# FFN in passes of three and six blocks, with gate and up of the six as seven half-size products of float16 pairs

## The chip, the cores and the metric

One core of one Trainium2 chip runs the whole program. The metric is device time in microseconds (us) of one launch; beside it a profile of one execution gives the span from the first to the last instruction and every instruction in it. The engines are TensorE (PE: matmuls, PEld: its weight loads), VectorE (DVE), ScalarE (ACT), GpSimd (POOL) and SyncE (SP, which here mostly issues DMAs).

## The reference

One step of a hybrid backbone: a layer with an attention head group and an mLSTM head group side by side, one output projection, then a SwiGLU FFN. There are 1152 tokens: 128 of context and 1024 latent. They make nine blocks of 128 rows; D_MODEL is 1024 and D_FF is 2816.

```python
def swiglu(h, w_gu, w_down):
    g, u = jnp.split(h @ w_gu, 2, axis=-1)
    return (jax.nn.silu(g) * u) @ w_down

# trunk_layer, cut
mix = jnp.concatenate([attn_o, hm], axis=-1) @ w_out
x = x + g1 * mix
h2 = rmsnorm(x, norm2_w) * (1 + sc2) + sh2
x = x + g2 * swiglu(h2, w_gu, w_down)
# and at the end
y = rmsnorm(x, final_norm_w)
```

Attention has 8 query heads of 64 and 2 key heads; a latent token reads 1152 keys, a context token 128. The inputs and outputs are float32.

## The kernel before

**Precision.** A float32 product is made of three matmuls on pairs: an operand is split into a high part and a low part, and high x high, high x low and low x high are added in PSUM. In the FFN and the output projection both parts are float32r; in the input projections they are float16.

**Tiling.** The nine blocks go through the FFN in three passes ("chunks" c = 0, 1, 2) of CB = 3 blocks, 384 tokens (CT). D_FF is cut into 22 slices f of 128. For a slice, `gate_up` loads two pieces of weights of 128x1024 (`load_piece`: DMA into `raw`, ACT casts the high part `whi` at L163, DVE subtracts for the low part `wlo` at L141), and for each runs 8 x 3 matmuls with 384 columns (L1436 to L1438). ACT (tanh) and DVE (L1455, L1456) form silu(g) * u, which is split into `hl`. `down` follows each group of slices (GROUPS): for each half n of the 1024 outputs, weight pieces of two slices each and three matmuls of 512 columns a slice and block (L1192 to L1194); the result goes through `add_gated` (two DVE operations of 512, L1181 and L1182) onto the rows `x1`. So every FFN weight is loaded and split three times, once a pass.

**Beside the passes.** Attention of chunk c + 1 runs woven into the pass of chunk c. A head is six score matmuls S (L1112) into one PSUM buffer of three banks, a maximum on DVE (L1114), an exponent on ACT (L1115), a float16 high part on ACT (L1118) and low part on DVE (L1119), two DMA transposes on SP's queue, and, for two heads at a time, value matmuls (L1136, L1137). `attn_out` applies the attention half of the output projection (8 pieces of `w_out` in two passes, 4 each; 72 matmuls), and `norm2` normalises, transposes and splits the next chunk's features during the last `down` of a pass. Before the first pass `prefill` does the mLSTM half of the output projection for all nine blocks, with part of chunk 1's attention woven in. The last group's `down_last` normalises each block as soon as it is complete and stores it.

**What sets the order.** Each engine executes its own instructions in the order of the program; that order is fixed before by a scheduler that takes the written order as priorities, `hot(n)` raising some, and readiness by a timeline. `weave(main, side, n_main, n_side)` draws n_side steps of a side generator evenly over n_main units of the main one. Buffers rotate by tag: `raw` has two, the split pieces five pairs (tags wl, ipair1, ipair0, iraw0, wq), PSUM four banks for general use (`bank`), one for values and three for S.

Of the kernel before, what the change touches and what calls it, by code (L numbers as in the profile page):

```python
# [19 lines left out]
P = 128  # L20
# [17 lines left out]
LAST = [(0, 5), (5, 5), (10, 4), (14, 4), (18, 4)]  # L38
PAIRS = [(0, 1), (2, 3), (4,), (5, 6), (7, 8)]
NG = 4  # L40
# [6 lines left out]
def hybrid_step(ctx: ExitStack, tc: tile.TileContext, I: dict, O: dict):  # L47
# [98 lines left out]
    def load_piece(srcs, shape, raw=None, own=None):  # L146
# [7 lines left out]
        raw = wp.tile([P, 1024], F32, name=nm("raw"), tag="iraw1", bufs=2) if raw is None else raw  # L154
        if not own:
            loaded["n"] = (loaded["n"] + 1) % 5
            tag = ("wl", "ipair1", "ipair0", "iraw0", "wq")[loaded["n"]]
            at = homes.get(tag, wp)
            own = [at.tile([P, 1024], F32R, name=nm(t), tag=tag, bufs=2) for t in ("whi", "wlo")]
# [4 lines left out]
        sub(lo[:, :n], raw[:, :n], hi[:, :n].bitcast(F32), "dve")  # L164
        return view(hi), view(lo)
# [253 lines left out]
    hp = ctx.enter_context(tc.tile_pool(name="hpk", bufs=1, side="right", reuse_waits="tile"))  # L419
# [644 lines left out]
    ap = ctx.enter_context(tc.tile_pool(name="ap", bufs=1, side="right", reuse_waits="tile"))  # L1064
    ap2 = ctx.enter_context(tc.tile_pool(name="ap2", bufs=1, side="right", reuse_waits="tile"))
    psum["S"] = ctx.enter_context(tc.tile_pool(name="pS", bufs=1, space=PSUM, reuse_waits="tile"))
    es_d = ExitStack()
    for name, bufs in (("mm", 3), ("wi", 2)):
        psum[name] = (ctx if name == "mm" else es_d).enter_context(tc.tile_pool(name="p" + name, bufs=bufs, space=PSUM, reuse_waits="tile"))
# [84 lines left out]
    def a_tiles():  # L1154
        return (hp.tile([P, KD, CT], F32R, name=nm("aTh"), tag="b2"),
                hp.tile([P, KD, CT], F32R, name=nm("aTl"), tag="b3"))

    def new_x1(c):
        x1 = (hp if c == 1 else rowp).tile([P, CB, D], F32, name=nm("x1"), tag="b5" if c == 1 else "b4")
        for i in range(CB):  # L1160
            if c == 2:
                dma(x1[:, i, :], x1_d[i])
        return [x1[:, i, :] for i in range(CB)]
# [11 lines left out]
    def t2():  # L1175
        return ft.tile([P, 512], F32, name=nm("t2"), tag="t2", bufs=3)
# [31 lines left out]
    def out_gates():  # L1208
        gs = []
        for n in range(2):  # L1210
            gl = xg.tile([P, 512], F32, name=nm("gl"), tag=("gl", "gx")[n], bufs=1)
            dma(gl, g_d[0, 1:2, n * 512 : (n + 1) * 512].to_broadcast([P, 512]))
            gs.append(gl)
# [161 lines left out]
    def attn_out(a, oT, gs):  # L1375

        ws = [out_pieces(0, n) for n in range(2)]
        x1 = a["x1"]
# [307 lines left out]
```

## Time and profile before

| what | value |
|---|---|
| median of 3 runs | 1529.32 us (1527.43 to 1531.47) |
| span of the profiled execution | 1523.0 us |
| PE busy, share of the span | 1466.2 us, 96% |
| DVE busy | 1017.2 us, 67% |
| ACT busy | 771.3 us, 51% |
| POOL busy | 268.0 us, 18% |
| granted TensorE clock, mean | 0.994 |

The profiled execution is known by its span; a time of its own besides is not listed, and the runs' median lies 6.3 us above the span. Busy times are sums over an engine's instructions; a matmul's busy time overlaps that of the next, so that the step between starts, not the busy time, tells its pace. In the slices of the page each digit is the busy share of a fortieth of the span in tenths. A row of the groups gives the line, engine, operation, tiles, shapes and count, then busy time, mean ns of one, and the idle time before with what ended it. A row of windows gives the window, its length, then each engine's busy time (and count), the granted clock, the DMA engines' share and GB/s; with one line chosen, only that line's busy time stands there.

### The profile page before, as it was taken

The page shows a single profiled execution, that of the slowest core. Times are in us where ns is not written, and L with a number is a line of the kernel's source. Part 1 is how long each engine was busy: PE and PEld are TensorE (multiplying, and loading weights), DVE is VectorE, ACT ScalarE, POOL GpSimd, SP SyncE. Part 2 cuts the span into 40 slices and gives each one's busy share as a digit, 9 for nine tenths or more (in the row PEclk, how much of TensorE's full clock was granted, in tenths as well). Part 3 has the DMA queues.
Part 4 walks back from the last instruction along what each step waited for, and adds up shares of the span by engine and source line. Part 5 has one row for each costly group of instructions (what it writes and reads, how often), then busy time and mean ns, then how long its engine had stood idle before and what let it go on. Part 6 is the DMA issues. An engine that isn't in the chain of part 4 may idle for free.

```text
span 1523.0 us, 23411 instructions
## 1 busy us (share of the span) xinstructions
PE 1466.2 (96%) x8539; PEld 1239.4 (81%) x8539; DVE 1017.2 (67%) x2021; ACT 771.3 (51%) x1433; POOL 268.0 (18%) x354
## 2 busy tenths in 40 slices
PE   6889999999998899999999999999999999999997
PEld 3635667677776789989998999989998989999996
DVE  4979555838567966877647487787866585554554
ACT  4855576847654644646433344656553443323333
POOL 0122422333344531000010100100010101101110
PEclk9999999999999999999999999999999999999998
DMA  9575223523465676878635366986864455543541
GB/s 368 162 224 189 73 70 42 123 55 78 104 187 189 149 195 176 197 168 192 166 113 164 125 206 192 198 183 143 193 145 140 137 153 172 153 141 123 152 144 56
DMA packets 386665, 233.77 MB, mean 153 GB/s; under 512 B 169142, under 2 KB 345478, under 8 KB 386550
## 3 DMA queue, kind: packets, MB, share of 16 engines
q1 hardware_dynamic: 384414, 228.62, 55.3%
q10 hardware_dynamic: 2008, 3.26, 1.0%
q8 instruction: 67, 1.10, 0.3%
q14 instruction: 48, 0.39, 0.1%
q0 software_dynamic: 128, 0.39, 0.1%
HBM read 182.21 MB, written 11.69 MB: 127 GB/s over the span
## 4 chain that ended last, share of the span: by engine, by line
PE 59%; DVE 2%; DMA 1%; ACT 0%; issue 0%; SPq 0%; DVEq 0%
PE mm L1438 11%; PE mm L1437 11%; PE mm L1436 11%; PE mm L1192 5%; PE mm L1193 5%; PE mm L1194 5%; PE S L1112 3%; PE po L1137 1%; PE po L1136 1%; DMA plT<-pl 1%; PE mm L1224 1%; PE mm L1220 1%; PE mm L1222 1%; DVE t L1181 0%; DVE x L1182 0%; PE mm L120 0%
## 5 line engine op out<-in xcount | busy, mean ns | idle before, releaser
L163 ACT CAST whi<-raw 128x1024 fp32r<-128x1024 f32 x214 | 219.1, 1025 | 365.7 <-PE mm L1437 129.8
L141 DVE TENSOR_TENSOR wlo<-raw,whi 128x1024 fp32r<-128x1024 f32 x214 | 257.7, 1204 | 176.0 <-ACT whi L163 173.0
L1437 PE MATMUL mm<-aTl,whi 128*128 128x384 f32 x1056 | 354.4, 336 | 0.0
L1438 PE MATMUL mm<-aTh,wlo 128*128 128x384 f32 x1056 | 354.2, 336 | 0.0
L1436 PE MATMUL mm<-aTh,whi 128*128 128x384 f32 x1056 | 353.2, 335 | 0.0
L141 POOL TENSOR_TENSOR hl<-tn,hl 128x384 fp32r<-128x384 f32 x66 | 83.5, 1267 | 848.6 <-ACT hl L1459 792.4
L1436 PEld LDWEIGHTS mm<-aTh,whi 128*128 128x128 f32 x1056 | 198.3, 188 | 0.7
L1437 PEld LDWEIGHTS mm<-aTl,whi 128*128 128x128 f32 x1056 | 198.3, 188 | 0.6
L1438 PEld LDWEIGHTS mm<-aTh,wlo 128*128 128x128 f32 x1056 | 198.3, 188 | 0.4 <-issue 0.4
L1192 PE MATMUL mm<-whi,hl 128*128 128x512 f32 x372 | 144.4, 392 | 1.1 <-DVE t L1181 1.1
L1193 PE MATMUL mm<-wlo,hl 128*128 128x512 f32 x372 | 145.1, 391 | 0.0
L1194 PE MATMUL mm<-whi,hl 128*128 128x512 f32 x372 | 142.7, 391 | 0.0
L1119 DVE SCALAR_TENSOR_TENSOR pl<-pr,st,ph 128x1152 f16<-128x1152 f32 (+1 forms) x72 | 98.0, 1361 | 37.1 <-ACT ph L1118 37.0
L1114 DVE TENSOR_REDUCE st<-S 128x1 f32<-128x1152 f32 (+1 forms) x72 | 88.9, 1234 | 16.8 <-PE S L1112 16.5
L1115 ACT ACTIVATE pr<-S,st 128x1152 f32<-128x1152 f32 (+1 forms) x72 | 81.3, 1129 | 35.0 <-DVE st L1114 30.8
L1118 ACT ACTIVATE ph<-pr,st 128x1152 f16<-128x1152 f32 (+1 forms) x72 | 83.8, 1164 | 26.5 <-issue 10.7
L510 PE MATMUL wi<-headw,hT 128*128 128x384 f16 x288 | 93.9, 326 | 0.2 <-ACT th L800 0.2
L511 PE MATMUL wi<-headw,hT 128*128 128x384 f16 x288 | 93.9, 326 | 0.0
L512 PE MATMUL wi<-headw,hT 128*128 128x384 f16 x288 | 93.9, 326 | 0.0
L1181 DVE TENSOR_TENSOR t<-mm,gl 128x512 f32<-128x512 f32 x102 | 69.1, 686 | 36.8 <-PE mm L1194 17.7
L1112 PE MATMUL S<-kst,qT 128*128 128x384 f32 (+1 forms) x400 | 84.5, 344 | 0.8 <-ACT pr L1115 0.8
L1192 PEld LDWEIGHTS mm<-whi,hl 128*128 128x128 f32 x372 | 69.9, 188 | 15.2 <-DVE t L1181 1.5
(401 smaller groups left out, 2588.6 us busy)
## 6 DMA issues: line engine op xcount, KB each, us to landing
raw<-in_w_gu_dram SPq DMA_DIRECT2D x132, 512.0 KB
raw<-in_w_down_dram SPq DMA_DIRECT2D x60, 512.0 KB
a<-in_w_ada_dram SPq DMA_DIRECT2D x24, 512.0 KB
gl<-g_d SPq DMA_DIRECT2D x36, 256.0 KB
iraw<-in_w_in_dram SPq DMA_DIRECT2D x32, 256.0 KB
x<-in_x_sample_dram SPq DMA_DIRECT2D x11, 512.0 KB
raw<-in_w_out_dram SPq DMA_DIRECT2D x10, 512.0 KB
aw<-in_w_ada_dram SPq DMA_DIRECT2D x8, 512.0 KB
```

The costliest lines, as they stand in the source:

```text
L141: (dve if eng == "dve" else pool).tensor_tensor(out=out, in0=full, in1=hi, op=ALU.subtract)
L163: nc.scalar.copy(hi[:, :n], raw[:, :n])
L510: mm(ps[:, :n], ah, wh[:, k % 2, c0 : c0 + n], start=(k == 0), stop=False)
L511: mm(ps[:, :n], ah, wl[:, k % 2, c0 : c0 + n], start=False, stop=False)
L1112: mm(S[:, n, 0:w], qT[:, h, :], kst[kv][:, t, c0 + n * w : c0 + (n + 1) * w], start=(t == 0), stop=(t == 1))
L1119: dve.scalar_tensor_tensor(out=plv, in0=prv, scalar=st[:, 3:4], in1=phv, op0=ALU.mult, op1=ALU.subtract)
L1192: mm(ps, ah, wh[:, k % 2, :], start=(k == 0), stop=False)
L1193: mm(ps, ah, wl[:, k % 2, :], start=False, stop=False)
L1194: mm(ps, al, wh[:, k % 2, :], start=False, stop=(k == nk - 1))
L1436: mm(ps, wh[:, k, :], th[:, k, :], start=(k == 0), stop=False)
L1437: mm(ps, wh[:, k, :], tl[:, k, :], start=False, stop=False)
L1438: mm(ps, wl[:, k, :], th[:, k, :], start=False, stop=(k == KD - 1))
```

## The change

The three passes become two: the first of three blocks as before, and one of six (chunks 1 and 2 together, `SIX` = groups of 4, 4, 4, 4, 3, 3 slices).

- **Seven products.** For a slice, gate and up weights are cut along their 1024 inputs into halves and make a 2x2 block matrix (A11 and A12 of gate, A21 and A22 of up); the features of chunk 1 (B11, B21) and chunk 2 (B12, B22) make the other. `pair6` computes the 2x2 product from seven half-size products (4 steps of 128 inputs x 3 matmuls, 384 columns) instead of eight, with sums of weights (`weights6`, on DVE) and sums of features (`features6`) formed before, and sums of results after, some of them by adding a product onto a bank that already holds one (products 4, 5, 6 onto banks a, d, c).
- **Float16 pairs.** Both operands of these products are scaled by powers of two and split into float16 parts. The features' scale comes from the modulation (`six_scales`), that of the weights from the sums of absolute values taken by ACT for every piece in the first pass (`tally`), reduced in `weight_scale` between the passes.
- **Attention of six beside the first pass.** `attention_side` runs chunk 1's rest, its `attn_out`, chunk 2's attention and its `attn_out`, woven over the first three groups (12 slices) of the first pass (NG is 3; 92 steps instead of 50). `features6` for six blocks is woven into the last two groups (10 slices).
- **Buffers.** The attention pools are closed before the six-block pass; then `Bt` holds the features, `A4` (seven tiles) the weight pairs, `raw` has four tiles and the split down pieces four pairs; all eight PSUM banks serve `bank`. `down6` and `down_last` go over six blocks; gate vectors g2 are loaded once.

```diff
-LAST = [(0, 5), (5, 5), (10, 4), (14, 4), (18, 4)]
+SIX = [(0, 4), (4, 4), (8, 4), (12, 4), (16, 3), (19, 3)]
+PRODUCTS = ((A11, B11), (S2, T2), (S1, T1), (S3, T3), (A12, B21), (S4, B22), (A22, T4))
-NG = 4
+NG = 3
...
+        if tally is not None:
+            jk = ft.tile([P, D], BF16, name=nm("jk"), tag="t2", bufs=4)
+            act(jk[:, :n], raw[:, :n], AF.Abs, accum_out=wsum[:, tally : tally + 1])
...
+    def weight_scale():
+        dve.tensor_reduce(out=six[:, 7:8], in_=wsum, axis=AX.X, op=ALU.max)
+        emit(power_scale(fp, ones, six[:, 7:8], six[:, 2:4]))
+        dve.tensor_tensor(out=six[:, 4:5], in0=six[:, 1:2], in1=six[:, 3:4], op=ALU.mult)
...
+    def features6(a, c, i, Bt, firsts):
...
+        first = firsts.pop(0)
+        T = sp.tile([P, 4, 4, P], F32, name=nm("T"), tag="S", bufs=1)
+        with hot(600):
+            dve.tensor_tensor(out=T[:, T1], in0=first[:, 0:4], in1=F[:, 0:4], op=ALU.subtract)
+            dve.tensor_tensor(out=T[:, T2], in0=F[:, 4:8], in1=T[:, T1], op=ALU.add)
+            dve.tensor_tensor(out=T[:, T3], in0=F[:, 0:4], in1=F[:, 4:8], op=ALU.subtract)
+            dve.tensor_tensor(out=T[:, T4], in0=first[:, 4:8], in1=T[:, T2], op=ALU.subtract)
...
+    def weights6(f):
...
+        S = sp.tile([P, 4, 512], F32, name=nm("S"), tag="S", bufs=1)
+        dve.tensor_tensor(out=S[:, 1], in0=u[:, 0], in1=u[:, 1], op=ALU.add)
+        dve.tensor_tensor(out=S[:, 0], in0=u[:, 0], in1=g[:, 0], op=ALU.add)
+        dve.tensor_tensor(out=S[:, 2], in0=S[:, 1], in1=g[:, 0], op=ALU.add)
+        dve.tensor_tensor(out=S[:, 3], in0=S[:, 2], in1=g[:, 1], op=ALU.add)
+        ops = {}
+        for names, v in (((A11, A12), g), ((S2, S4), S[:, 2:4]), ((S3, S1), S[:, 0:2]), ((A22,), u[:, 1:2])):
+            n = len(names)
+            t = a4p.tile([P, 2, 2, 512], F16, name=nm("A"), tag="A4", bufs=7)
+            act(t[:, 0:n, 0], v, AF.Copy, scale=six[:, 2:3])
+            dve.scalar_tensor_tensor(out=t[:, 0:n, 1], in0=v, scalar=six[:, 2:3], in1=t[:, 0:n, 0], op0=ALU.mult, op1=ALU.subtract)
...
+    def pair6(f, Bt, acts):
+        ops = weights6(f)
+        a, b, c, d = (bank()[:, 0:CT] for _ in range(4))
+        def product(n, ps, first):
+            (wh, wl), bt = ops[PRODUCTS[n][0]], Bt[:, PRODUCTS[n][1]]
+            for k in range(4):
+                mm(ps, wh[:, k], bt[:, 0, k], start=first and k == 0, stop=False, skip_group_check=True)
+                mm(ps, wh[:, k], bt[:, 1, k], start=False, stop=False, skip_group_check=True)
+                mm(ps, wl[:, k], bt[:, 0, k], start=False, stop=k == 3, skip_group_check=True)
...
+        product(0, a, True)
+        nc.scalar.copy(p1, a)
+        product(1, b, True)
+        dve.tensor_tensor(out=u2, in0=b, in1=p1, op=ALU.subtract)
+        product(2, d, True)
+        product(3, c, True)
+        dve.tensor_tensor(out=u3, in0=c, in1=u2, op=ALU.add)
+        dve.tensor_tensor(out=c22, in0=u3, in1=d, op=ALU.subtract)
+        product(4, a, False)
+        act(tn[:, 0], a, AF.Tanh, scale=six[:, 5:6])
+        product(5, d, False)
+        dve.tensor_tensor(out=gb, in0=d, in1=u2, op=ALU.subtract)
+        act(tn[:, 1], gb, AF.Tanh, scale=six[:, 5:6])
+        dve.scalar_tensor_tensor(out=tn[:, 1], in0=tn[:, 1], scalar=1.0, in1=c22, op0=ALU.add, op1=ALU.mult)
+        dve.tensor_tensor(out=tn[:, 1], in0=tn[:, 1], in1=gb, op=ALU.mult)
+        product(6, c, False)
+        dve.tensor_tensor(out=c21, in0=c, in1=u2, op=ALU.add)
+        dve.scalar_tensor_tensor(out=tn[:, 0], in0=tn[:, 0], scalar=1.0, in1=c21, op0=ALU.add, op1=ALU.mult)
+        dve.tensor_tensor(out=tn[:, 0], in0=tn[:, 0], in1=a, op=ALU.mult)
+        act(hl[:, 0], flat, AF.Copy, scale=six[:, 6:7])
+        dve.scalar_tensor_tensor(out=hl[:, 1], in0=flat, scalar=six[:, 6:7], in1=hl[:, 0].bitcast(F32), op0=ALU.mult, op1=ALU.subtract)
...
+    def down6(x1, acts, f0, nf, gs):
+        for n in range(2):
+            pieces = down_pieces6(f0, nf, n)
+            for i in range(2 * CB):
+                ps = bank()
+                down_block6(ps, pieces, acts, i)
+                add_gated(x1[i], ps, gs[n], n)
...
+    def attention_side():
+        yield from six_scales()
+        yield from att
+        yield from attn_out(nxt, oT, lambda: row_pair(g_d[0, 1]))
+        o2 = []
+        yield from attention(2, o2, set())
+        yield from attn_out(far, o2, lambda: row_pair(g_d[0, 1]))
+    main = groups(0, cur, GROUPS[:NG])
...
+    side = attention_side()
+    weave(main, side, 18 * sum(nf for _, nf in GROUPS[:NG]) - 24, 92)
+    emit(side)
+    es_att.close()
...
+    main = groups(0, cur, GROUPS[NG:])
+    weave(main, feats, 18 * sum(nf for _, nf in GROUPS[NG:]), 40)
+    emit(feats)
+    weight_scale()
...
+    for f0, nf in SIX:
+        acts = []
+        for f in range(f0, f0 + nf):
+            for _ in pair6(f, Bt, acts):
+                if f > 0:
+                    next(done6, None)
+        if (f0, nf) != SIX[-1]:
+            emit(down6(x6, acts, f0, nf, gs6))
+        else:
+            down_last(x6, acts, f0, nf, gs6)
```

280 lines of the change are left out of this document (190 added, 90 removed).

## The prediction

> **What bounds the kernel now.** I read the page's busy shares first, then its slices, then windows over the stages.
>
> ```profile
> PE 1466.2 (96%) x8539; PEld 1239.4 (81%) x8539; DVE 1017.2 (67%) x2021; ACT 771.3 (51%) x1433; POOL 268.0 (18%) x354
> ...
> PE   6889999999998899999999999999999999999997
> DVE  4979555838567966877647487787866585554554
> ```
>
> PE has work in nearly every slice; DVE is second, and uneven. Where the change lies, I cut the span at the first gate and up matmuls of each pass. Windows over the three stages, and one inside the second (PE, PEld, DVE, ACT, POOL busy, granted clock, DMA share, GB/s):
>
> ```profile
> 560.00:889.00 329.00, 328.43 (x1810) 303.78 (x1809) 220.09 (x312) 151.89 (x199) 30.31 (x24) 1.00 0.65 166
> 889.00:1235.00 346.00, 343.21 (x1915) 316.51 (x1913) 253.83 (x377) 174.33 (x234) 27.35 (x22) 1.00 0.67 168
> 1235.00:1523.00 288.00, 276.83 (x1467) 260.23 (x1467) 156.03 (x225) 99.66 (x137) 28.61 (x22) 0.99 0.45 138
> 930.00:1140.00 210.00, 207.76 (x1204) 191.95 (x1203) 162.59 (x226) 119.03 (x155) 16.52 (x13) 1.00 0.77 174
> ```
>
> One gate and up line, 352 matmuls in each pass:
>
> ```profile
> 560.00:889.00 329.00, 118.27 (x352) 1.00 0.65 166
> 889.00:1235.00 346.00, 117.63 (x352) 1.00 0.67 168
> 1235.00:1523.00 288.00, 117.30 (x352) 0.99 0.45 138
> ```
>
> The score matmuls, six a head:
>
> ```profile
> 450.00:560.00 110.00, 10.06 (x48) 1.00 0.65 178
> 560.00:889.00 329.00, 19.83 (x96) 1.00 0.65 166
> 889.00:1235.00 346.00, 29.67 (x144) 1.00 0.67 168
> ```
>
> PE idles only 963 - 948.5 = 14.5 us after 560 us, most of it in the tail. So PE bounds all three passes. At six S matmuls a head, chunk 1's attention does 8 of its 24 heads before 560 and 16 in the first pass; chunk 2's 24 lie in the second pass; the third pass is FFN alone.
>
> A busy PE row overstates a matmul, so I take the step from start to start: float32r with 384 columns (first and last of 17 rows), float16 with 384 columns (of 21), and float32r with 512 columns (of 24).
>
> ```profile
> 1339.80 0.33 PE L1437 MATMUL mm<-aTl,whi 128*128 128x384 f32 x1
> 1342.58 0.33 PE L1438 MATMUL mm<-aTh,wlo 128*128 128x384 f32 x1
> ```
> ```profile
> 324.81 0.33 PE L512 MATMUL wi<-headw,hT 128*128 128x384 f16 x1
> 328.06 0.33 PE L511 MATMUL wi<-headw,hT 128*128 128x384 f16 x1
> ```
> ```profile
> 1495.83 0.39 PE L1524 MATMUL mm<-whi,hl 128*128 128x512 f32 x1
> 1501.09 0.39 PE L1526 MATMUL mm<-whi,hl 128*128 128x512 f32 x1
> ```
>
> The steps are 2.78/16 = 173.7 ns, 3.25/20 = 162.5 ns and 5.26/23 = 229 ns. A pass is 1056 x 0.1737 + 396 x 0.229 = 183 + 91 = 274 us of PE; of it one f (a 128-wide slice of D_FF) is 12.5 us. The second pass's other 69 of 343 us are attention: 16.5 us are the 72 output projection matmuls, 2.6 us the transposes of norm2 (24 at an estimated 0.11), and 50 are 24 heads, 2.1 us each.
>
> **The change, part by part.**
>
> *Gate and up of six blocks.* Before, 2 x 1056 = 2112 matmuls at 173.7 ns, 366.9 us. After, per f seven products of 4 x 3 = 84 matmuls, 1848 in all, in float16 with the same 384 columns: 300.3 us. So -66.6 us, of which 264 fewer matmuls make 45.9 and the shorter step 20.7. The down products stay 792 matmuls.
> The step is bounded by 162.5 ns (the row of the same shape and type, with nothing between its matmuls) and by float32r's own 173.7; I take the first.
>
> *DVE beside it.* These rows give the prices.
>
> ```profile
> L141 DVE TENSOR_TENSOR wlo<-raw,whi 128x1024 fp32r<-128x1024 f32 x202 | 249.5, 1235 | 162.2 <-ACT whi L163 159.2 <-PE mm L1224 2.4
> L1119 DVE SCALAR_TENSOR_TENSOR pl<-pr,st,ph 128x1152 f16<-128x1152 f32 x64 | 94.9, 1483 | 35.1 <-ACT ph L1118 35.0
> L1114 DVE TENSOR_REDUCE st<-S 128x1 f32<-128x1152 f32 x64 | 86.6, 1353 | 13.7 <-PE S L1112 13.5
> L1181 DVE TENSOR_TENSOR t<-mm,gl 128x512 f32<-128x512 f32 x102 | 69.1, 686 | 36.8 <-PE mm L1194 17.7 <-DMA gl<-g_d 10.4 <-PE mm L1526 6.5
> L1182 DVE TENSOR_TENSOR x<-x,t 128x512 f32<-128x512 f32 x72 | 48.7, 687 | 0.7
> L1455 DVE SCALAR_TENSOR_TENSOR tn<-tn,mm 128x384 f32<-128x384 f32 x66 | 36.4, 552 | 54.2 <-PE mm L1438 54.0
> L235 DVE SCALAR_TENSOR_TENSOR ipair<-iraw,isc,ipair 128x1024 f16<-128x1024 f32 x2 | 2.5, 1264 | 0.0
> L163 ACT CAST whi<-raw 128x1024 fp32r<-128x1024 f32 x202 | 211.7, 1050 | 337.2 <-PE mm L1437 118.5 <-DMA raw<-in_w_gu_dram 110.2 <-PE mm L1193 65.2
> L1118 ACT ACTIVATE ph<-pr,st 128x1152 f16<-128x1152 f32 x64 | 80.6, 1259 | 25.3 <-issue 10.7 <-ACT pr L1115 5.9 <-DVE st L1117 2.8
> L1141 DVE SCALAR_TENSOR_TENSOR oT<-po,vsc,ol 64x128 f32<-64x128 f32 x48 | 16.4, 341 | 4.1 <-ACT ol L1139 3.5
> ```
>
> Per f the six-block stage asks DVE for four sums of 512 (4 x 0.687), low parts of 3.5 x 1024 float16 (3 x 1.264 + 0.75), nine operations of 384 (9 x 0.552) and one of 768 (1.0, between the 512 and the 1024 rows): 2.75 + 4.54 + 4.97 + 1.0 = 13.3 us, beside 84 x 0.1625 = 13.65 us of PE. With 22 down pieces (27), 72 gated additions of two operations (99), the first pass's finish (5) and the last stage (13) the sum is 292 + 144 = 436 us of DVE beside 300.3 + 181.4 = 481.7 us of PE, 91%. The A4 ring of seven tiles lets DVE work 1.75 f ahead during a down phase, so its total fits. Within an f, product 5 adds to bank d and waits for c22, two operations (1.1 us and the hops) behind product 3, and only product 4 (12 x 0.1625 = 1.95 us) covers them. A 1.26 us operation already running on DVE breaks that cover. Bounds: 0 when the order puts the next f's products between, 22 x 2.5 = 55 us when both operations come late behind two others each time. I take 10 us (some 0.5 us an f), near the lower end, because PE lost 2 us in 210 at 77% DVE load (the window 930 to 1140).
>
> *Attention of six beside 12 f of the first pass.* PE work: 12 x 12.5 + 40 heads x 2.1 + 2 x 16.5 = 267 us. DVE work: 44 pieces x 1.235 (36 FFN, 8 of w_out) = 54, 30 gated additions x 1.37 = 41, tanh products 24 x 0.552 = 13, 40 heads x 3.66 (1.353 + 1.483 + 0.31 for two small ones + 0.34 for oT + 0.17 for qT) = 146, rest 7: 262 us, 98% of PE's. PE work here only moves from the second pass; what is new is that DVE's slack is gone. How full can DVE run?
>
> ```profile
> 875.00:900.00 25.00, 25.00 (x133) 22.40 (x132) 24.55 (x53) 13.70 (x20) 0.00 (x0) 1.00 0.52 157
> 500.00:525.00 25.00, 21.79 (x121) 17.86 (x120) 23.53 (x62) 16.20 (x27) 12.41 (x10) 1.00 0.59 129
> 675.00:700.00 25.00, 25.00 (x141) 23.12 (x140) 22.48 (x33) 14.22 (x18) 1.18 (x1) 1.00 0.88 203
> ```
>
> Up to 98% for 25 us, and 90 to 94% in windows that lie in attention. I take 92%: 262/0.92 = 285, so +18 us. Bounds: 0 (DVE at 98%), and +42 (at 85%). The tally (absolute sums of 1024, estimated at the cast's 1.05 us; 24 of the 44 lie here) goes to ACT, which has room: 40 heads at some 3.0 (two passes of 1152 and small ones) = 120, 44 casts 46, tally 25, rest 21, together 212 us in 267. Transposes (two a head) and loads share SP's queue; a load of 512 KB takes 0.45 x 288/66 = 1.96 us of all DMA engines (third pass), so a head takes (0.77 x 210 - 38 x 1.96)/24 = 3.6, and 40 heads with 44 loads ask for 230 of 285 us, 81%. The window with 0.88 kept PE full, so nothing is added. A transpose that waits for `pl` holds the weight loads queued behind it; 0 taken, some us if two raw buffers run dry. The remaining 10 f (125 us of PE) cover features6: DVE 69 + 36 us.
>
> *Fewer loads.* Weights of gate, up and down are read twice instead of three times. DMA, and ACT's casts, are hidden already in the third pass (share 0.45), so 0.
>
> *The seam.* `weight_scale` needs the whole first pass's tally, goes through PE twice, and every product waits for the cast scaled by it. The same steps stand early in the trace, with the clock after them.
>
> ```profile
> 41.34 0.27 PE L120 MATMUL mm<-ident,hbd 128*1 128x128 f32 x1 [0.86 <-DVE hbd L426]
> 43.52 0.43 PE L190 MATMUL mm<-pv,one 1*128 1x2 f32 x2 [1.90 <-DVE pv L179]
> 45.97 0.41 PE L510 MATMUL wi<-ipair,hT 128*128 128x272 f16 x1 [2.03 <-ACT hT L534]
> ```
> ```profile
> 44.00:46.00 2.00, 0.03 (x1) 0.50 1.06 388
> 46.00:48.00 2.00, 1.69 (x7) 0.50 1.10 371
> 48.00:50.00 2.00, 2.00 (x10) 0.50 1.09 348
> ```
>
> From the transpose to the first product are 4.6 us, with the 1.26 us operation for the low part behind it 5 to 6. Here PE had run little for 6 us, and the clock stood at 0.50 for 6 us: 3 us lost if that repeats. Bounds: 0 (hidden in the last 20 us of down products) to 9. I take 6.
> The Trainium skill ("TensorE: Matmul & The Clock Gate", Part 1) says that PE falls to half rate after an idle window of about 3.4 us and needs as long a busy one to come back. By that rule a seam with 5 us idle costs 5 + 1.7 = 6.7 us (an estimate from that page), and the sum would be 0.7 us longer; the trace agrees in kind, with 0.50 behind the gap.
>
> *The tail.* With three f, a block is 18 x 0.229 = 4.1 us of PE and 4 x 0.687 + 0.68 + 0.75 + small = 5 us of DVE, so DVE sets the end: +3 us (bounds 0 and 8: six blocks at 0.9 us, and late last sums).
>
> Sum against the profiled span: 1523.0 - 66.6 + 10 + 18 + 6 + 3 = 1493.4 us. The runs' median lies 1529.32 - 1523.0 = 6.3 us above the span; kept, that is 1499.7, so **1500 us**.
>
> **The rivals.**
>
> *PE keeps all of it.* The order hides DVE's load as in the window 875 to 900; only 3 us of the seam and 3 of the tail stay: 1523.0 - 66.6 + 6 + 6.3 = 1469 us. For it: PE lost 3.4 us in 560 to 1235. Against: DVE was there at 70%, not at 91 and 98.
>
> *Slower: DVE becomes the bound.* Then the stretch and the six-block stage last DVE work over attainable load e: (262 + 436)/e instead of 267 + 481.7 = 749. With seam and tail the gain is used up at 698/e = 749 + 57.6, e = 0.865. At e = 0.85 they last 821 us, 72 more: 1523.0 - 66.6 + 72 + 9 + 6.3 = 1544 us. For it: chained work, scores to maximum to exponent to low part with one S buffer; the window 500 to 525 has DVE at 94% and PE at 87%. Against: that window is the prefill stage, whose own chain (transposes, POOL's additions) also holds PE.
>
> *The step doesn't shrink.* Should float16 operands of this layout run at 173.7 ns, 20.8 us go back: 1521 us, a gain of half a percent. Against: the rows above, same shape.
>
> **How the numbers follow.** Likeliest, 1500 (1483 to 1521): 0.52. All of the gain, 1469: 0.24. DVE the bound, 1544: 0.16, some of it between 1525 and 1534. Unshrunk step or an equal mix near the old time: 0.08. Changes under 0.3% (4.6 us: the three runs spread over 4.04 us) count as the same. Faster 0.79, same 0.06, slower 0.15. The range 1466 to 1540 holds the first two cases, the fourth, and the near part of the third.
>
> **What would show it.** Right: product lines at 0.163 us steps, 1848 of them; DVE near 90% or more in the first 270 to 300 us after 560; the six-block stage about 490 us; a hole of some 5 us at the seam, with the clock dipping. Wrong: PE waits on DVE in product 5 or 6 summing to tens of us; score matmuls spaced over 8 us so that attention outlasts the 12 f; PE waiting for casts or raw loads.

## The result, and the profile after

The changed kernel is slower. Its median is 1594.67 us (1590.41 to 1597.2, four runs) beside 1530.39 for the kernel before on the same chip: a ratio of 1.0419, with a 95% interval of 1.0396 to 1.0443. The prediction of 1500 us and its range of 1466 to 1540 us both missed. The experiments below ran on chips where the kernel before takes 1525 to 1527 us, so kernels are compared by their ratios to it: there the changed kernel's 1.0419 stands for about 1590 us. "Points" are hundredths of that ratio, 15.3 us each.

The page of the changed kernel, its busy shares and slices:

```profile
PE 1453.9 (91%) x8281; PEld 1078.4 (68%) x8281; DVE 1131.8 (71%) x2272; ACT 817.0 (51%) x1524; POOL 210.7 (13%) x310
...
PE   6899999999988999669975799998999999999995
DVE  4978556657488857665875567778969687786856
...
PEclk9899999999999999769996799998999999999997
```

TensorE has two troughs that the kernel before had not, in the 17th and 18th and the 21st to 23rd of the 40 slices (a slice is 40 us), and the granted clock falls in both. They lie in the first pass. Windows over the stretch with attention (first FFN slices to the last `attn_out` block), the rest of the first pass with the seam, and the six-block stage (PE, PEld, DVE, ACT, POOL busy, granted clock, DMA share, GB/s):

```profile
560.00:945.00 385.00, 316.90 (x1598) 267.13 (x1597) 250.07 (x368) 210.10 (x289) 17.32 (x14) 0.88 0.64 144
945.00:1086.80 141.80, 133.27 (x720) 123.91 (x719) 102.31 (x171) 85.53 (x137) 13.81 (x10) 0.99 0.47 139
1086.80:1594.10 507.30, 487.36 (x2640) 328.83 (x2640) 393.95 (x628) 176.98 (x236) 0.00 (x0) 0.98 0.25 75
```

The sum of the prediction gave these three 285, 125 + 6 = 131, and 1493.4 - 560 - 285 - 131 = 517 us. So the first is 100 us too long, the second 11, and the third 10 shorter; together 101 us, the miss of the span (1594.1 against 1493.4). What has to be explained lies mainly in the 385 us, and DVE, which the prediction made their bound, is busy for 250 of them, 65%.

The same windows finer: a stretch with heads beside FFN, and the two troughs; first all engines, then the score matmuls (six a head), then one of the three gate and up lines (16 matmuls a slice).

```profile
647.00:712.00 65.00, 43.35 (x186) 33.09 (x187) 43.47 (x63) 35.94 (x47) 2.19 (x2) 0.68 0.60 121
...
754.00:833.00 79.00, 71.46 (x402) 65.05 (x402) 63.50 (x88) 56.25 (x78) 5.49 (x5) 0.98 0.88 194
833.00:918.00 85.00, 55.26 (x240) 41.56 (x241) 49.08 (x74) 41.33 (x53) 0.00 (x0) 0.72 0.58 107
...
647.00:712.00 65.00, 21.20 (x66) 0.68 0.60 121
...
754.00:833.00 79.00, 12.61 (x60) 0.98 0.88 194
833.00:918.00 85.00, 23.29 (x78) 0.72 0.58 107
...
560.00:611.00 51.00, 22.01 (x64) 1.00 0.72 205
...
647.00:712.00 65.00, 2.80 (x8) 0.68 0.60 121
712.00:754.00 42.00, 10.97 (x32) 0.97 0.36 92
754.00:833.00 79.00, 21.45 (x64) 0.98 0.88 194
833.00:918.00 85.00, 0.00 (x0) 0.72 0.58 107
```

From 754 to 833 there are 10 heads and four slices' gate and up, and TensorE is busy for 71.46 of 79 us. In the troughs there are 11 and 13 heads and next to no FFN. Their work at full clock, estimated as busy time x mean clock, is 43.35 x 0.68 + 55.26 x 0.72 = 69 us in 150 us: 81 us lost over 24 heads, 3.4 us each. Of the 12 slices' 192 matmuls of this line, 64 (four slices) ran before 611 us, where only two heads stand, and 32 beside `attn_out` of chunk 1.

What TensorE waited for in 560 to 1110 us, the three largest:

```profile
PE S L1127 <- ACT pr L1130: 27.7, 11, 3.0
PE po L1152 <- DMA plT<-pl: 16.1, 13, 2.6
PE po L1151 <- DMA phT<-ph: 8.3, 3, 4.8
```

The 27.7 us on the score buffer (the first row) all lie in the two troughs, and so do 23.2 of the 24.4 us on the two transposes. So about half of the 51 us that TensorE idles there is a wait for the score buffer; most of the rest is a wait of the value matmuls for the transposes.

The chain of one head in the second trough, from the timeline (start, duration): scores, maximum, exponent, next head's scores.

```profile
855.41 2.27 PE L1127 MATMUL S<-kst,qT 128*128 128x384 f32 x6
...
857.72 1.36 DVE L1129 TENSOR_REDUCE st<-S 128x1 f32<-128x1152 f32 x1 [0.71 <-PE S L1127]
...
859.11 1.22 ACT L1130 ACTIVATE pr<-S,st 128x1152 f32<-128x1152 f32 x1 [1.56 <-DVE st L1129]
...
860.47 1.73 PE L1127 MATMUL S<-kst,qT 128*128 128x384 f32 x6 [2.79 <-ACT pr L1130]
```

There is one score buffer, so the next scores wait until the exponent has read the last ones: 860.47 - 855.41 = 5.1 us for this head. From 839.03 to 905.71 us the scores of 13 heads start, 5.6 us apart on the mean (the expectations below use 5.8). TensorE's own share of a head is 2.1 us at full clock. Without FFN to run in the wait it idles, 2.8 us at this place, and the clock goes down.

### The profile page after: what moved, and what is told of

Read it like the earlier page. It is cut to its first block, busy times and chain, and to the rows that moved or that the text cites. A ratio compares the mean times of both kernels' runs of the same rounds, so it can differ in the third digit from the quotient of the medians.

```text
span 1594.1 us, 22742 instructions
## 1 busy us (share of the span) xinstructions
PE 1453.9 (91%) x8281; PEld 1078.4 (68%) x8281; DVE 1131.8 (71%) x2272; ACT 817.0 (51%) x1524; POOL 210.7 (13%) x310
## 5 line engine op out<-in xcount | busy, mean ns | idle before, releaser
L1612 PE MATMUL mm<-Bt,A 128*128 128x384 f16 x616 | 200.8, 329 | 3.7 <-ACT A L1598 3.7
L1613 PE MATMUL mm<-Bt,A 128*128 128x384 f16 x616 | 202.5, 329 | 0.0
L1614 PE MATMUL mm<-Bt,A 128*128 128x384 f16 x616 | 198.2, 328 | 0.0
L144 DVE TENSOR_TENSOR wlo<-raw,whi 128x1024 fp32r<-128x1024 f32 (+1 forms) x102 | 122.2, 1198 | 58.5 <-ACT whi L173 54.5
L173 ACT CAST whi<-raw 128x1024 fp32r<-128x1024 f32 (+1 forms) x102 | 103.1, 1013 | 117.7 <-DMA raw<-in_w_down_dram 47.2
L1465 PE MATMUL mm<-aTh,whi 128*128 128x384 f32 x352 | 119.7, 341 | 2.1 <-DVE tn L1485 1.0
L1467 PE MATMUL mm<-aTh,wlo 128*128 128x384 f32 x352 | 119.8, 341 | 0.5 <-DVE wlo L144 0.4
L1466 PE MATMUL mm<-aTl,whi 128*128 128x384 f32 x352 | 119.3, 339 | 0.0
L1127 PEld LDWEIGHTS S<-kst,qT 128*128 128x128 f32 x400 | 79.7, 217 | 37.4 <-ACT pr L1130 34.5
L1612 PEld LDWEIGHTS <-A 128*128 128x128 f16 x616 | 60.5, 98 | 47.4 <-ACT A L1598 4.5
L144 POOL TENSOR_TENSOR hl<-tn,hl 128x384 fp32r<-128x384 f32 x22 | 27.5, 1253 | 469.0 <-ACT hl L1488 444.1
L1598 ACT ACTIVATE A<-S,six 128x1024 f16<-128x1024 f32 x44 | 50.2, 1147 | 73.8 <-PE mm L1614 59.3
L1614 PEld LDWEIGHTS <-A 128*128 128x128 f16 x616 | 60.4, 98 | 40.4 <-issue 0.5
L1613 PEld LDWEIGHTS <-A 128*128 128x128 f16 x616 | 60.5, 98 | 39.5 <-issue 0.8
```

The lines of the kernel that those rows point to most:

```text
L144: (dve if eng == "dve" else pool).tensor_tensor(out=out, in0=full, in1=hi, op=ALU.subtract)
L173: nc.scalar.copy(hi[:, :n], raw[:, :n])
L1127: mm(S[:, n, 0:w], qT[:, h, :], kst[kv][:, t, c0 + n * w : c0 + (n + 1) * w], start=(t == 0), stop=(t == 1))
L1465: mm(ps, wh[:, k, :], th[:, k, :], start=(k == 0), stop=False)
L1466: mm(ps, wh[:, k, :], tl[:, k, :], start=False, stop=False)
L1467: mm(ps, wl[:, k, :], th[:, k, :], start=False, stop=(k == KD - 1))
```

## The experiments

An **uncovered** head is one with under 1 us of gate, up or down matmuls ahead of the next head. How many there are can be counted in the order of TensorE's instructions, which is fixed before the run: 23 of the last 40 heads in the changed kernel, none in the kernel before. The tables give that count.

### First set: which resource

**e1_17f**: attention drawn over 17 slices.
```diff
-NG = 3
+NG = 4
-    weave(main, side, ... - 24, 92)
+    weave(main, side, ... - 24, 70)
```


> Edit: NG 4 instead of 3 and 70 side steps instead of 92, so attention of six is drawn over 17 slices f of the first pass instead of 12; features over the last 5 instead of 10; all work the same. In the order of PE's instructions 12 of the 40 heads stand with no FFN matmul between them and the head before, against 23 in the changed kernel. Theory T1 (a head's chain of scores, maximum, exponent with one S buffer needs some 5.8 us alone and some 8.5 beside FFN, of which PE uses 2.1; 12 f are too little FFN for 40 heads, and a head without FFN beside it leaves PE idle): each such head costs about 122/23 = 5.3 us, so 11 fewer give 1594 - 58 = 1536 us. T2 (DVE's throughput is the bound, as the prediction had it): DVE's work is unchanged, 1594 us within 10. T3 (the halved clock makes the loss): clock in 650 to 900 back near 1 only where the heads have FFN beside them; same sign as T1, no separate number.

Measured 1581.11 us, ratio 1.036 (1.0334 to 1.0387): 0.6 points or 9 us better. T1's 58 us did not come; the number is within T2's 10 us. The trace shows why fewer uncovered heads won so little: ten of them, with scores from 884.43 to 957.50 us, stand 7.3 us apart instead of 5.6. From 885 to 960 us TensorE waits there not only for the score buffer but as long again for a transpose:

```profile
PE po L1151 <- DMA phT<-ph: 16.4, 5, 3.9
PE S L1127 <- ACT pr L1130: 16.2, 5, 4.6
```

So an uncovered head has no fixed price. At 7.3 - 2.1 = 5.2 us, 12 of them lose an estimated 62 us, where the changed kernel lost 81.

**e2_pool**: DVE relieved.
```diff
-        sub(lo[:, :n], raw[:, :n], hi[:, :n].bitcast(F32), "dve")
+        sub(lo[:, :n], raw[:, :n], hi[:, :n].bitcast(F32), "pool" if <every second gate or up piece of the first pass> else "dve")
```


> Edit: in the first pass the low part of every second gate or up piece goes to POOL instead of DVE (22 pieces, some 27 us of DVE less, 12 of them beside attention); order of heads nearly as in the changed kernel (22 heads without FFN). T2 (DVE throughput): 12 x 1.235/0.92 = 16 us faster or more, up to 29, about 1570. T1 (chain of the heads, too little FFN beside): within 8 us of 1594, since DVE idles in the stretches that lose the time.

Measured 1601.18 us, 1.0505 (1.0471 to 1.0539): slower by 13 us, which neither expectation had and which wasn't taken apart. The troughs are the same with DVE at 63% of the time, so DVE's throughput isn't the bound there. (Next to no FFN pieces lie in the troughs, so the edit took little of DVE's work from them.)

```profile
647.00:712.00 65.00, 38.73 (x175) 30.88 (x173) 40.52 (x58) 33.50 (x43) 5.50 (x3) 0.70 0.56 114
833.00:918.00 85.00, 55.11 (x237) 41.89 (x236) 54.73 (x81) 43.04 (x56) 2.03 (x2) 0.70 0.61 121
```

**e3_nohold**: `attn_out`'s weights not through the ring of five pairs, its blocks in the value bank; `w_out` isn't loaded for attention, and features stand in its place.
```diff
-        ws = [out_pieces(0, n) for n in range(2)]
+        ws = [[<views of the features cur["h2"]>] * 2 for n in range(2)]
-        ps = bank()                      # in out_block and q's transposes
+        ps = psum["po"].tile(...)
```


> Edit: attn_out takes its weights from tiles that are there already (the first pass's features) instead of loading w_out through the ring of five split pairs, so the two attention halves of the output projection are computed with wrong weights; and attention's transposes and attn_out's blocks use the value bank instead of FFN's four banks. Matmul counts unchanged, 8 loads, casts and low parts left out. 19 heads without FFN stand in PE's order, against 23. Rival T4 (the loss comes from FFN waiting for pairs and banks that attn_out holds): most of the 122 us back, near 1490. T1: FFN still has only 12 f to offer, 1594 - 4 x 5.3 = 1573, some us less for the left out loads.

Measured 1634.32 us, 1.0695 (1.0662 to 1.0729). T4 falls, and T1's 1573 us failed too. At the end of attention 14 heads in a row stood uncovered, 7.5 us apart (scores from 849.06 to 946.05 us), and from 845 to 947 us TensorE waits 24.4 us for `phT` and 19.0 for the score buffer.

**e4_20f**: 20 slices, chunk 1's `attn_out` at once, value bank as above.
```diff
-GROUPS = [(0, 4), (4, 4), (8, 4), (12, 5), (17, 5)]
+GROUPS = [(0, 4), (4, 4), (8, 4), (12, 4), (16, 4), (20, 2)]
-    side = attention_side()                # first 3 groups, 92 steps
+    side = chain(six_scales(), att, whole(attn_out(nxt, ...)), attention(2, o2, set()))   # first 5, 70 steps
```


> Edit: GROUPS cut to 4,4,4,4,4,2 slices; attention of six and the two attn_out (each at once, not spread) drawn over the first 20 slices, features over the last 2; attention's transposes and attn_out's blocks in the value bank. All work the same. 7 heads without FFN. T1: 16 fewer heads at 5.3 us give -85 us, and the features, 36 us of DVE beside only 25 us of PE, cost 15 to 25 back: 1524 to 1534 us, about the kernel before. T2: 1594 within 10. T4: also faster, no separate number.

Measured 1592.61 us, 1.0444 (1.0416 to 1.0473). Only 8 heads were uncovered on the chip, yet nothing was won. With two slices left, the last `attn_out` and `features6` stood almost alone: from 985 to 1085 us TensorE was busy for 62 of 100 us. So a count of heads across kernels that differ in buffers and in what comes last tells little. The next set changes the count within one set of buffers.

### Second set: the number of uncovered heads

All four share these edits: chunk 1's `attn_out` at once, the value bank for it and for q's transposes, six `oT` tiles paid for by one `pr` tile and four `hl` tiles, and groups of 4, 4, 4, 4, 3, 3 slices in the first pass. They differ in the slices that attention is drawn over (with the number of side steps set to match: 92, 92, 62 and 55), and in whether chunk 1's attention is moved ahead, beside the mLSTM stage:
```diff
-    att = attention(0, oT, done, 200, 100)
-    weave(head_project(0, sts[0]), beside((att, 0.1),), 96, 96)
+    att = chain(attention(0, oT, done, 200, 100), attention(1, o1, set(), 200, 100))
+    weave(head_project(0, sts[0]), beside((att, 0.2),), 96, 96)
...
-        weave(head_project(h, sts[h]), beside((scan, 0.42), (att, 0.11)), 96, 96)
+        weave(head_project(h, sts[h]), beside((scan, 0.42), (att, 0.22)), 96, 96)
```


> Control for the next three: this order written with chunk 2's attention drawn over the first 12 slices, attn_out of chunk 1 at once in the value bank, four hl tiles instead of five, one pr tile instead of two, six oT tiles; chunk 1's attention where the changed kernel has it. In the written order 18 heads of the first pass stand with no gate, up or down matmul before the next head (changed kernel 23, and 26 of 41 on the chip). T5 (uncovered heads): a covered head takes about 6.3 us of FFN and 2.1 of its own, an uncovered one 5.8 us and more with 2.1 of PE work, so each costs 3.7 to 5 us; all covered would be about 1500, so 18 give about 1581 us. T6 (attention beside the first pass costs 114/41 = 2.8 us a head, covered or not): 1594, as the changed kernel.

> As e5_c3, with the attention drawn over 16 slices and features6 over the last 6. 12 uncovered heads in the written order. T5: 1500 + 12 x 4.5 = 1554 us. T6: 1594.

> As e5_c3 (12 slices), but all of chunk 1's attention is drawn twice as fast beside the mLSTM stage, straight behind chunk 0's, so that 24 heads are left for the first pass; 7 of them uncovered in the written order. T5: 1500 + 7 x 4.5 = 1531 us. T6: 16 fewer heads, 1594 - 45 = 1549, the same as e8_z1. T7 (the earlier stages have no room either: a head moved there costs its 5.8 us there): 1590 or more.

> As e7_b3, with chunk 2's attention over 16 slices: no uncovered head in the first pass. T5: the loss of about 95 us (26 heads at 3.7) goes, 1500 us (1490 to 1520), faster than the kernel before. T6: 1549. T7: 1590 or more.

| run | moved ahead | slices | uncovered | ratio (95%) |
|---|---|---|---|---|
| e5_c3 | no | 12 | 18 | 1.0836 (1.0806 to 1.0866) |
| e6_c4 | no | 16 | 12 | 1.0630 (1.0603 to 1.0657) |
| e7_b3 | yes | 12 | 7 | 1.0563 (1.0525 to 1.0600) |
| e8_z1 | yes | 16 | 0 | 1.0316 (1.0291 to 1.0341) |

Each step goes the way of the count: e5 to e6 is 31 us for 6 heads, e7 to e8 38 for 7, e6 to e8 48 for 12, e5 to e7 42 for 11; 3.8 to 5.4 us a head. T6 would have e5 equal to e6 and e7 to e8; the two steps that move heads would fit it as well (16 heads at 2.8 us are 45). The level, though, is some 75 us over T5's: with 18 uncovered heads e5 is 64 us slower than the changed kernel with 23. That goes with the shared edits and wasn't taken apart. In part it is a dearer uncovered head, as in e1 and e3: in e5 the last ten stand 7.5 us apart (892.94 to 960.78 us), and TensorE's largest wait in 560 to 1170 us is one of 8.3 us in the changed kernel:

```profile
PE po L1151 <- DMA phT<-ph: 46.9, 13, 8.6
```

### Third set: the move with the changed kernel's own buffers

Chunk 0's `oT` goes through DRAM instead of staying in its tiles, so that three do; `pr`, `hl` and the banks are the changed kernel's; chunk 1's `attn_out` is at once again.
```diff
                         if j == 3:
                             done.add(i)
+                            if c == 0: dma(o_d[i], oT[i])
...
-                        nc.scalar.copy(th, oT[i])
+                        dma(x1[:, i, 0:512], o_d[i]); nc.scalar.copy(th, x1[:, i, 0:512])
```


> Chunk 1's attention beside the mLSTM stage as in e7_b3, but with the changed kernel's buffers: chunk 0's oT goes through DRAM so that three oT tiles do, and pr, hl and the banks are as in the changed kernel. 12 slices of FFN for chunk 2's attention; 6 uncovered heads in the written order instead of 23. T5: the changed kernel's 1594.7 less about 20 heads x 3.7 = 74, plus up to 28 that the mLSTM stage lost in e8_z1: 1521 to 1549 us. T6 (2.8 us a head in the first pass, covered or not): 1549; so T6 is told apart by the next run. T7 (the earlier stages lose what the first pass wins): 1585 or more.

> As e9_early12 with 16 slices for chunk 2's attention (no uncovered head in the written order) and 6 for features6. T5: 6 x 4.5 = 27 us under e9_early12, 1500 to 1525 us. T6: the same as e9_early12. T8 (features6 needs the ten slices, its DVE work of 105 us standing beside 75 us of FFN): 10 to 30 us over T5.

> As e10_early16, but about 16 of chunk 1's 24 heads beside the mLSTM stage and 8 left for the stage before the first pass; 2 uncovered heads. T5: within 10 us of e10_early16, lower if the mLSTM stage lost there by crowding (28 us in e8_z1 with all 24).

> As e10_early16, but chunk 1's attn_out stands ahead of the first pass's weave and its blocks, like the transposes of q, use the value bank. In the written order the first head of chunk 2 then stands 8 us into the FFN instead of 44. If the FFN spent ahead of the heads is what is lacking at the end: 10 to 20 us under e10_early16. If blocks that wait for each other in one bank cost more (PE waited 7 to 8 us for them in e4_20f and e8_z1): over it.

| run | slices | uncovered | ratio (95%) |
|---|---|---|---|
| e9_early12 | 12 | 6 | 1.0361 (1.0338 to 1.0383) |
| e10_early16 | 16 | 0 | 1.0191 (1.0169 to 1.0213) |
| e11_part16 (weights 0.15, 0.16) | 16 | 2 | 1.0003 (0.9987 to 1.0019) |
| e12_bank16 (`attn_out` first, value bank) | 16 | 1 | 1.0276 (1.0257 to 1.0296) |

e9 to e10 is 26 us for 6 heads, 4.3 each, as T5 said. But both lie over 30 us above the upper end of T5's range, and e11, with two more uncovered heads, is 29 us faster than e10: the move itself costs, where too many heads crowd the mLSTM stage. One window from 150 to 470 us, of e10 and then of e11:

```profile
150.00:470.00 320.00, 298.40 (x1915) 215.49 (x1914) 217.36 (x519) 216.56 (x530) 86.92 (x172) 0.97 0.52 99
```
```profile
150.00:470.00 320.00, 311.37 (x2041) 227.30 (x2038) 217.00 (x525) 219.81 (x579) 108.98 (x210) 0.99 0.51 100
```

e10 gets 126 fewer matmuls done there (1915 against 2041), in 13 us less busy time and at a lower clock. So T7 holds in part: 24 of chunk 1's heads crowd the earlier stages more than 16 do. Other numbers weren't run. e12 is 13 us over e10; in 560 to 1100 us its largest wait of TensorE is of blocks that follow each other in the one value bank:

```profile
PE po L1248 <- DVE t L1201: 7.1, 7, 1.7
```

### Fourth set: the chain and the other terms

**e13_seam**
```diff
             yield from down(c, a, f0, nf, 0)
+            if f0 + nf == NF: weight_scale()
             yield from down(c, a, f0, nf, 1)
...
     emit(feats)
-    weight_scale()
```


> The changed kernel with weight_scale written ahead of the last down half of the first pass instead of behind it; nothing else. In the written order its two small matmuls then stand 36 down matmuls ahead of the first product. The prediction's term: the seam costs 6 us, so 6 us less than the changed kernel, about 1589 us (1585 to 1592). If the seam's hole is set by something else (features, the first weights): within 2 us of 1594.7.

Measured 1590.19 us, 1.0419 (1.0404 to 1.0435): the same ratio as the changed kernel, so the seam's 6 us were not won; with both intervals up to some 4 us could hide. (The time itself lies within the expected 1585 to 1592 us, but so does the changed kernel's 1590 us on this chip.) Ten us around the seam, of the changed kernel and of e13:

```profile
1080.00:1090.00 10.00, 3.76 (x14) 1.56 (x13) 8.71 (x24) 7.58 (x11) 0.00 (x0) 0.65 0.46 142
```
```profile
1074.00:1084.00 10.00, 5.84 (x22) 2.89 (x20) 6.98 (x15) 5.06 (x8) 0.00 (x0) 0.83 0.44 131
```

The hole shrinks from 6.2 us idle to 4.2. What is left is the first weights' own path: TensorE still waits 3.3 us for the cast A.

**e14_eighth**
```diff
+        product(7, b, True)
         product(2, d, True)
```


> The changed kernel with an eighth product of the size of the others for every slice (12 more matmuls onto bank b, 264 in all), its result left unused. If TensorE bounds the six-block stage: 264 x 162.5 ns = 43 us more, 1638 us. If DVE bounds it (25.00 of 25 us busy in several windows): 0 to 15 us more.

Measured 1630.39 us, 1.0680 (1.0666 to 1.0695): 2.61 points or 40 us over the changed kernel, for the 43 expected of TensorE. It is full there (one product line, and a window inside the stage):

```profile
L1613 PE MATMUL mm<-Bt,A 128*128 128x384 f16 x704 | 230.7, 328 | 0.0
...
1125.00:1580.00 455.00, 455.00 (x2509) 305.75 (x2507) 325.94 (x481) 138.79 (x171) 0.00 (x0) 1.00 0.21 63
```

**e15_nomax**: attention without its maximum.
```diff
-                    dve.tensor_reduce(out=st[:, 0:1], in_=Sv, axis=AX.XY, op=ALU.max, negate=True)
-                    act(prv, Sv, AF.Exp, bias=st[:, 0:1], accum_out=st[:, 1:2])
+                    act(prv, Sv, AF.Exp, scale=2.0 ** -7, accum_out=st[:, 1:2])
```


> The changed kernel with attention's maximum left out (the exponent takes the scores times 2^-7 and no bias; the attention is not that of the reference): one step of the head's chain, 1.35 us on DVE, is gone. 16 uncovered heads in the written order instead of 23, and 3 to 5 us of FFN beside a covered head instead of 5 to 8. T5, with the head's own chain as what sets its pace: an uncovered head takes 4.3 us instead of 5.8, so 7 x 3.7 + 16 x 1.5 = 50 us less, 1545 us (1535 to 1560). If transposes or loads set the pace instead: 1580 or more.

Measured 1532.87 us, 1.0040 (1.0026 to 1.0054): 3.79 points, 58 us less than the changed kernel, for the 50 expected. Windows with all engines, then with the score matmuls, of a covered stretch and of the second trough:

```profile
727.00:803.00 76.00, 73.93 (x434) 67.03 (x433) 54.12 (x83) 59.41 (x83) 5.60 (x4) 1.00 0.98 219
...
727.00:803.00 76.00, 15.29 (x72) 1.00 0.98 219
...
803.00:850.00 47.00, 33.74 (x172) 26.81 (x172) 25.92 (x50) 32.38 (x44) 1.26 (x1) 0.82 0.83 147
...
803.00:850.00 47.00, 15.17 (x61) 0.82 0.83 147
```

The scores of the uncovered heads start from 801.82 to 844.29 us, ten steps of 4.25 us, where the changed kernel has 5.56 (839.03 to 905.71): 1.3 us less for a step of 1.36 us, with as many transposes and loads as before. So the chain sets the pace of an uncovered head. DVE, which loses the work too, wasn't full in either trough (25.92 of 47 us here). Covered heads take 76/12 = 6.3 us instead of 79/10 = 7.9, but TensorE is busy for 73.93 of the 76 us, so their pace is the FFN that the order puts beside each; that is less here (3 to 5 us instead of 5 to 8). The 58 us hold both the shorter chain and the smaller count of uncovered heads (16 instead of 23).

**e16_cover**: e11 with 75 steps instead of 62, and e13's edit.

> As e11_part16, with the side work drawn a little faster (75 steps instead of 62: no uncovered head at the end in the written order) and weight_scale ahead of the last down half. T5: e11_part16's 1527.0 less 2 x 4.5 for the two heads and less 6 for the seam: 1512 us (1507 to 1518), faster than the kernel before by 0.6 to 1.2%. If the two heads' time only moves to the features: 1521.

Measured 1517.21 us (five runs), 0.9943 (0.9929 to 0.9956): faster than the kernel before, by 9 us or 0.6%, and 73 us under the changed kernel by the ratios. Its slices, and windows over most of chunk 2's attention with all engines, the score matmuls and one gate and up line:

```profile
PE 1423.9 (94%) x8281; PEld 1064.8 (70%) x8281; DVE 1136.5 (75%) x2282; ACT 812.8 (54%) x1522; POOL 219.3 (14%) x310
...
PE   6889999999998889999999989989999999999994
...
PEclk9899999999999999999999999999999999999997
...
695.00:893.00 198.00, 191.30 (x1088) 174.34 (x1087) 153.33 (x214) 132.97 (x186) 15.58 (x12) 0.99 0.80 184
...
695.00:893.00 198.00, 28.64 (x138) 0.99 0.80 184
...
695.00:893.00 198.00, 58.67 (x174) 0.99 0.80 184
```

23 heads in 198 us, 8.6 us each, beside 174/16 = 11 slices, and the troughs are gone. It is 5 us over T5's 1512 and within its range. Several things differ from the changed kernel at once, among them the heads moved ahead, `attn_out` at once, attention over 16 slices and the earlier `weight_scale`.

**e17_before_part**: the kernel before with e11's move alone (weights 0.15 and 0.16, chunk 0's `oT` through DRAM).

> The kernel before with the move of e11_part16 alone: chunk 1's attention drawn earlier, beside the mLSTM stage (0.15 and 0.16 steps a step instead of 0.1 and 0.11, straight behind chunk 0's), and chunk 0's oT through DRAM. Three passes, no seven products. If e16_cover's gain comes from the two passes and their products: within 4.6 us of the kernel before, since TensorE was full there with or without the move, or up to 15 us slower from the crowding of the mLSTM stage. If it comes from the move: 0.6% faster.

Measured 1542.23 us, 1.0104 (1.0084 to 1.0123): 16 us slower than the kernel before. So in the kernel before the move is a price, not a gain. If it costs as much in e16, which no run shows, the two passes with seven products are worth some 25 us there and not 9 (an estimate).

**e18_warm**: matmuls to keep the clock up.
```diff
                     Sv = S[:, 0:parts, 0:w]
+                    if c == 2 and i >= 1:
+                        ps = bank()
+                        for k in range(12): mm(ps[:, 0:CT], qT[:, h, :], kst[kv][:, 0, 0:CT], ...)
```


> The changed kernel with 12 matmuls of 384 columns, whose result nobody reads, behind the scores of each of chunk 2's last 16 heads (some 2.1 us of TensorE a head at full clock). Read by the distance of uncovered heads, 5.8 us in the changed kernel at a granted clock of 0.50 to 0.81. T3 (the reduced clock is part of the head's chain: six score matmuls take 2.0 to 2.3 us instead of 1.05 to 1.2): with TensorE kept busy the clock stays near 1.00 and uncovered heads stand 4.7 to 5.0 us apart. If the clock is only a sign of the idle time: 5.8 or more, since the dummies stand in line ahead of the next scores.

One run of 1597.92 us. The order put the extra matmuls mostly where heads were covered or behind one another in blocks of 28, and the uncovered heads that remained had few of them. From 833 to 918 us the clock was at 0.96 instead of 0.72, but with other work beside nearly every head there. What the clock adds to an uncovered head stays open.

## Why the prediction was wrong, step by step

- **The step that failed** is "Attention of six beside 12 f of the first pass", at its question "How full can DVE run?". It took 262 us of DVE work over an attainable 92% and got 285 us, +18; the stretch took 385, with DVE at 65%. Where the time was lost, no engine's throughput sets the pace but the latency of a head's chain: scores, maximum and exponent through one score buffer, and behind them the transposes that the value matmuls wait for. What DVE and TensorE could do together was never asked of them there, because no FFN stood in the chain's gaps. e15 (one chain step less, 1.3 us less an uncovered head), the pairs e5 and e6, e7 and e8, e9 and e10 (4.3 to 5.4 us a head) show it, and e16 (no troughs, 73 us less) fits; in e2 less work for DVE won nothing.
- **The rows were there.** The prediction's window 930 to 1140, with TensorE full, is nearly all of chunk 2's attention in the kernel before (23 of its 24 heads start in it). The scores of its first and last head:

```profile
926.20 1.21 PE L1112 MATMUL S<-kst,qT 128*128 128x384 f32 x6
...
1119.69 1.22 PE L1112 MATMUL S<-kst,qT 128*128 128x384 f32 x6
```

  That is 193.5/23 = 8.4 us a head, 2.1 of them its own, so 6.3 us of FFN. Twelve slices have 12 x 12.5 = 150 us, at this pace enough for 24 heads and not for 40. The other 16 at the 3.4 us measured here make 54 us in place of 18. On the chip it was 24 heads and 81 us, because FFN was also spent where hardly a head stands (four slices before 611 us, two beside `attn_out`). Against its 267 us of TensorE's work the stretch lost 118 us: the 81, some 17 us of idle time outside the troughs, and some 20 that are not taken apart. The prediction used that very window, but for what a transpose asks of the DMA queues and for how little TensorE lost at that load of DVE.
- **What the rows don't say** is that 12 slices could never be enough. The 6.3 us are what that order put beside a head, not what a head needs: 5.8 did in this kernel from 754 to 833 us, and an uncovered head loses 3.4 us. At 3.4 us a head, 40 heads would ask for 136 of the 150 us (an estimate). No run spreads 12 slices evenly over 40 heads, so how much of the loss is too little FFN and how much is FFN in the wrong place stays open.
- **Gate and up of six, -66.6 us**: right. First and last of 26 rows in the six-block stage:

```profile
1299.78 0.33 PE L1613 MATMUL mm<-Bt,A 128*128 128x384 f16 x1
...
1303.84 0.33 PE L1614 MATMUL mm<-Bt,A 128*128 128x384 f16 x1
```

  The step is 4.06/25 = 162.4 ns for the 162.5 assumed, and a product line has 616 matmuls, 1848 in all; e14 prices 264 more at 40 us.
- **DVE beside it, +10 us for products 5 and 6**: no loss at all. DVE's work in the stage is 394 us, for the 436 summed. In 450 us of the stage TensorE is never idle, with DVE at 78%:

```profile
1100.00:1550.00 450.00, 450.00 (x2474) 302.97 (x2473) 351.47 (x522) 153.25 (x189) 0.00 (x0) 1.00 0.25 74
```
- **The seam, +6 us**: the hole is 6.2 us idle at a clock of 0.65, as forecast, but only part of it is `weight_scale` (e13).
- **The tail, +3 us (0 to 8)**: too small. The last 33 us of the kernel before and of the changed kernel:

```profile
1490.00:1523.00 33.00, 22.35 (x107) 19.16 (x105) 15.93 (x40) 10.13 (x22) 1.95 (x2) 0.88 0.12 48
```
```profile
1561.10:1594.10 33.00, 13.58 (x59) 10.61 (x57) 26.17 (x72) 15.06 (x37) 0.00 (x0) 0.76 0.25 96
```

  At full clock that is 19.7 and 10.3 us of TensorE's work: 9 us. With the 10 us of DVE that didn't come, the third stage would be 4 us shorter than forecast; the other 6 of its 10 are not taken apart.
- **The 6.3 us between span and median** did not carry over: in the changed kernel 1594.67 - 1594.1 = 0.6 us.
- **The rivals**: that the time would come out on the slower side was there, at 0.16, but its mechanism was DVE as the bound, with TensorE waiting for its throughput, and its price 1544 us. The sign of being wrong that came true is the second one listed: attention outlasting the 12 slices. But the uncovered heads stood 5.6 us apart, not "over 8": some 8 us is the pace of the covered ones, which cost next to nothing.

Not settled: what share of an uncovered head's loss is the reduced clock (the six score matmuls take 2.27 us in the trough above; e18 didn't tell), which of the shared edits made e5 to e8 some 75 us slower, and why an uncovered head takes 5.6 us in the changed kernel and 7.3 to 7.5 in e1, e3 and e5, beyond the waits for transposes named above.

## What to carry to other kernels

Work that is woven into other work has a pace of its own: read from a stretch where both run full how much of the main work stands beside one step of the side work, multiply by the steps, and compare with the main work that is there, before asking for any engine's share. That amount is what one order gave, so it warns and doesn't prove; what a step loses when it stands alone is the lower figure. When a schedule is shortened, find out which slices of the main work stand ahead of the first side step and which beside nothing; they are lost as cover. And where main work runs short, shorten the chain or move part of the side work to another full stage, only as far as that stage has room.

## What the runs showed of the hardware

In the second trough the granted clock falls again and again with no long gap before it. From 839 to 918 us TensorE waits 3.0 us at most at a time (2.79 in the chain above), and yet the clock comes back to 1.00 and drops to 0.50 five times. Four windows of 2 us show two of these drops:

```profile
858.00:860.00 2.00, 0.00 (x0) 0.00 (x0) 2.00 (x2) 0.89 (x1) 0.00 (x0) 1.00 0.67 127
862.00:864.00 2.00, 0.44 (x2) 0.14 (x1) 1.83 (x2) 0.72 (x2) 0.00 (x0) 0.50 1.30 107
868.00:870.00 2.00, 1.56 (x11) 1.20 (x8) 0.90 (x3) 1.43 (x2) 0.00 (x0) 1.00 0.00 0
876.00:878.00 2.00, 2.00 (x11) 1.42 (x10) 0.94 (x1) 1.03 (x1) 0.00 (x0) 0.50 1.06 199
```

Over the 85 us of the trough TensorE is busy for two thirds of the time, at a mean clock of 0.72. The Trainium skill ("TensorE: Matmul & The Clock Gate", Part 1) puts the fall at an idle window of about 3.4 us; the trace here agrees in kind, but waits of 3.0 us and less were enough. Of the 81 us lost in the two troughs an estimated 29 are matmuls at the lower clock (43.35 x 0.32 + 55.26 x 0.28).
